# A decoder layer's token mixer: split weights kept in DRAM for the later blocks

## The chip, the cores and the metric

The kernel runs on one core of one Trainium2 chip. The metric is the time of one execution on the device in microseconds (us), the median over runs. Engines are called TensorE (PE in the profile, PEld for its weight loads), VectorE (DVE), ScalarE (ACT), GpSimd (POOL) and SyncE (SP). DVE, ACT, PE and POOL compute; SP only issues DMA transfers, and POOL's queue is used for stores.

## The reference

One layer on x of 2048 tokens and 1024 features, float32, conditioned by a vector c that gives shifts, scales and gates (`mod`, from `mod_w`):

```python
h = modulate(rms_norm(x, norm1_g), shift1, scale1)
q, k, v, g, cb, cc, cx = split(h @ w_in)                 # 4 x 512 and 3 x 512 columns
q, k = rotary(q, positions), rotary(k, positions)
y_ret = group_rms_norm(retention_chunkwise(q, k, v)) * silu(g)
y_conv = group_rms_norm(cb * causal_dwconv(cc * cx))
x = x + gate1 * (concat(y_ret, y_conv) @ w_out)
h = modulate(rms_norm(x, norm2_g), shift2, scale2)
a, val = split(h @ w_up)
x = x + gate2 * ((silu(causal_dwconv(a) + b) * val) @ w_down)
return modulate(rms_norm(x, final_norm_g), *fmod)
```

## The kernel before

**Products in two parts.** x is held as [feature, token]. A float32 operand of the large products is the exact sum of two float32r parts, hi and lo, and a product is three matmuls, hi x hi, hi x lo and lo x hi, accumulated in PSUM (`mm3`, L232 to L236). So each weight has to be split before it is used. `split_w` (L83) does it for a piece of 128 x 1024: SP loads 512 KB into one of 3 `raw` tiles (L85, L86), ScalarE casts it into the first half of one of 4 `w` tiles (L88), and VectorE subtracts the cast from the raw piece into the second half (L89):

```python
raw = rawp.tile([128, 1024], F32, tag="raw", name=nm("raw"))
nc.sync.dma_start(raw, src)
w = whlp.tile([128, 2, 1024], F32R, tag="w", name=nm("w"))
S.copy(w[:, 0, :], raw)
V.tensor_tensor(w[:, 1, :], raw, w[:, 0, :].bitcast(F32), op=ALU.subtract)
```

**The order of the pieces.** `plan` (L93) lists all pieces in the order in which the products take them, and `get_w` splits up to two pieces ahead of the one that it hands out (`ahead`, one in the prologue). The token mixer goes through 4 blocks of 512 tokens (`for b in range(NB)`), and each block uses all its weights again: `w_tok` in 16 pieces (q, k, v and gate, four each), `w_conv` in 12, `w_out` in 8. The pieces of k in block 0 are not in the plan; they are split at L562 to L566 into activation tiles of their own. A piece is 24 large matmuls. The channel mixer after it runs in two halves of 1024 tokens with `w_up` and `w_down`.

**One block.** v, k and q are projected (`proj_step`, L330), v is scaled (L319), k and q are rotated on VectorE straight out of PSUM (`rotary`, L302, its last step a product at L312 to L314), the gate comes out of ScalarE. Then four chunks of retention (`Retention`) alternate with four groups of the short convolution (`Conv`). In `values` the product of k and v goes into the PSUM tile `misc` (L399), which the transposes of the chunk before held until `back` has read it on ScalarE (L433) and VectorE (L434). While this runs, x of the next block is loaded (L500), squared (L211, L212), and its norm taken. `out_proj` (L474) multiplies by `w_out` in two groups of four banks. After each group VectorE takes the sums out of the banks and adds them to x (`xr`, loaded at L479, added at L489), POOL stores the result (L490). Between its 8 weight pieces `spread` (L605) places the normalised chunks of the next block's h: L229 multiplies x by the factor, L222 shifts on ScalarE, L215 and L216 split into `act`; and `more_mod` (L593), which loads four pieces of `mod_w` (L598) and sums them on VectorE (L163, then L165, L166, L170). The next block's first product needs the bank that the first L489 frees. In block 0 the modulation is computed first, with loads at L509 and the same L163, between the first products.

**Who sets the order.** Each engine works through its own list in order. The Tile framework's scheduler makes the lists from priorities, that is from the place in the program, and from the waits on tiles; only the prologue (L513) is written in a fixed order. SP's loads stand in one list too: one that waits for a free tile holds up those behind it.

## Time and profile before

| | |
|---|---|
| runs | 2412.23, 2409.52, 2411.40 us, median 2411.4 |
| span of the profiled execution | 2410.9 us (0.5 under the median) |
| TensorE, its weight loads | 2374.5 and 1953.8 us busy |
| VectorE | 1496.7 us busy |
| ScalarE | 837.1 us busy |
| POOL | 31.8 us busy |
| DMA | 239.53 MB, mean 99 GB/s |
| DMA share by 40 slices of 60 us, tenths | 8444633554264327311111111112511111111102 |

The span runs from the first to the last instruction that the profiler recorded; it is the profiled execution's own time, and the runs are other executions of the same kernel. The token mixer is the first 960 us, some 16 of the 40 slices; the rest is the channel mixer. In the rows, "<-" after an idle time names what ended it. PEclk is the granted clock of TensorE as a share of full speed. The mean of one matmul is larger than the distance of two starts, since they overlap; from a row of windows the count shows the pace.

### The profile page before, as it was taken

What the parts mean: (1) busy time and instruction counts of PE and PEld (TensorE: products, weight loads), DVE (VectorE), ACT (ScalarE), POOL (GpSimd) and SP (SyncE); (2) the same over time, 40 slices, a digit from 0 to 9 for tenths busy, and PEclk for the clock granted to TensorE, in tenths of its full rate; (3) what the DMA queues carried; (4) which work ended last, traced back from release to release, by engine and by line L of the source; (5) the groups of instructions that cost most, each with busy time, mean ns of one, the idle gap of its engine ahead of it and who ended that gap; (6) DMA issues with size and microseconds to landing.
All of it is one profiled execution on the core that took longest, in us unless ns stands there. A gap on an engine that the chain in (4) does not pass through costs nothing.

```text
span 2410.9 us, 27983 instructions
## 1 busy us (share of the span) xinstructions
PE 2374.5 (98%) x10954; PEld 1953.8 (81%) x10954; DVE 1496.7 (62%) x2755; ACT 837.1 (35%) x1234; POOL 31.8 (1%) x66
## 2 busy tenths in 40 slices
PE   8999999999999999999999999999999999999997
PEld 5888888887878887888888888888888888888887
DVE  8999759866986688644444444448844444444436
ACT  5255325523552355322222222234622222222234
POOL 0000000000000000000000000000100000000000
PEclk9999999999999999999999999999999999999999
DMA  8444633554264327311111111112511111111102
GB/s 306 143 131 131 232 113 114 175 187 142 71 216 150 114 86 268 101 53 53 41 47 53 53 36 52 53 53 71 191 54 45 43 53 53 44 44 53 53 27 71
DMA packets 88660, 239.53 MB, mean 99 GB/s; under 512 B 10240, under 2 KB 12304, under 8 KB 88528
## 3 DMA queue, kind: packets, MB, share of 16 engines
q1 hardware_dynamic: 84096, 223.71, 28.6%
q0 software_dynamic: 4288, 13.91, 1.5%
q8 instruction: 86, 1.41, 0.2%
q14 instruction: 46, 0.38, 0.0%
q10 hardware_dynamic: 144, 0.13, 0.0%
HBM read 219.88 MB, written 17.83 MB: 99 GB/s over the span
## 4 chain that ended last, share of the span: by engine, by line
PE 86%; DVE 7%; DMA 4%; issue 2%; ACT 1%; SPq 0%; POOL 0%; DVEq 0%; ACTq 0%; POOLq 0%
PE mm L234 20%; PE mm L236 20%; PE mm L235 20%; PE sc L234 4%; PE sc L235 4%; PE sc L236 4%; DMA x<-in_x 2%; PE y L234 2%; PE y L235 2%; PE y L236 2%; PE misc L234 2%; PE misc L235 2%; PE misc L236 2%; DMA x<-in_mod_w 1%; DVE w L89 1%
## 5 line engine op out<-in xcount | busy, mean ns | idle before, releaser
L234 PE MATMUL mm<-act,w 128*128 128x512 f32 x2048 | 801.7, 391 | 1.7 <-DVE xr L489 1.5
L235 PE MATMUL mm<-act,w 128*128 128x512 f32 x2048 | 798.4, 390 | 1.1 <-DVE act L216 1.1
L236 PE MATMUL mm<-act,w 128*128 128x512 f32 x2048 | 797.5, 389 | 0.0
L88 ACT CAST w<-raw 128x1024 fp32r<-128x1024 f32 x271 | 282.4, 1049 | 668.7 <-issue 362.9
L234 PEld LDWEIGHTS mm<-act,w 128*128 128x128 f32 x2048 | 384.8, 188 | 82.6 <-ACT act L215 3.4
L235 PEld LDWEIGHTS mm<-act,w 128*128 128x128 f32 x2048 | 384.8, 188 | 81.0 <-DVE act L216 2.1
L236 PEld LDWEIGHTS mm<-act,w 128*128 128x128 f32 x2048 | 384.7, 188 | 80.5
L89 DVE TENSOR_TENSOR w<-raw,w 128x1024 fp32r<-128x1024 f32 x271 | 328.4, 1220 | 120.8 <-ACT w L88 120.6
L234 PE MATMUL mm<-w,act 128*128 128x512 f32 x480 | 188.6, 394 | 8.3 <-DVE xr L489 4.4
L235 PE MATMUL mm<-w,act 128*128 128x512 f32 x480 | 188.0, 392 | 0.0
L236 PE MATMUL mm<-w,act 128*128 128x512 f32 x480 | 187.3, 393 | 0.0
L756 DVE SCALAR_TENSOR_TENSOR acc<-sc,mod,acc 128x512 f32<-128x512 f32 (+1 forms) x172 | 126.7, 737 | 83.3 <-PE sc L236 82.8
L729 DVE SCALAR_TENSOR_TENSOR fi<-a,cp,fi 128x512 f32<-128x512 f32 x88 | 66.1, 751 | 173.1 <-ACT fi L728 173.1
L741 DVE TENSOR_TENSOR fi<-fi,mm 128x512 f32<-128x512 f32 x88 | 60.5, 687 | 168.0 <-PE mm L236 167.3
L726 ACT COPY a<-mm 128x512 f32<-128x512 f32 x88 | 51.6, 587 | 316.1 <-PE mm L236 316.1
L235 PE MATMUL sc<-g,w 128*128 128x512 f32 (+1 forms) x348 | 134.4, 386 | 0.0
L234 PE MATMUL sc<-g,w 128*128 128x512 f32 (+1 forms) x348 | 134.4, 386 | 0.0
L236 PE MATMUL sc<-g,w 128*128 128x512 f32 (+1 forms) x348 | 134.3, 386 | 0.0
L234 PEld LDWEIGHTS mm<-w,act 128*128 128x128 f32 x480 | 90.5, 189 | 30.7 <-ACT act L215 10.3
L236 PEld LDWEIGHTS mm<-w,act 128*128 128x128 f32 x480 | 90.9, 189 | 19.2
L235 PEld LDWEIGHTS mm<-w,act 128*128 128x128 f32 x480 | 90.7, 189 | 19.0 <-DVE w L539 0.5
L732 DVE COPY ah<-a 128x2 f32<-128x2 f32 x44 | 7.4, 169 | 156.2 <-ACT a L726 156.2
(225 smaller groups left out, 2814.9 us busy)
## 6 DMA issues: line engine op xcount, KB each, us to landing
raw<-in_w_up SPq DMA_DIRECT2D x88, 512.0 KB, 3.6
raw<-in_w_tok SPq DMA_DIRECT2D x64, 512.0 KB, 5.3
x<-in_mod_w SPq DMA_DIRECT2D x96, 256.0 KB, 4.1
raw<-in_w_conv SPq DMA_DIRECT2D x48, 512.0 KB, 3.6
raw<-in_w_down SPq DMA_DIRECT2D x44, 512.0 KB, 3.6
raw<-in_w_out SPq DMA_DIRECT2D x32, 512.0 KB, 3.5
x<-in_x SPq DMA_DIRECT2D x56, 256.0 KB, 4.2
mw<-in_mod_w SPq DMA_DIRECT2D x32, 256.0 KB, 5.0
```

Source lines behind the costliest of these rows:

```text
L88: S.copy(w[:, 0, :], raw)
L89: V.tensor_tensor(w[:, 1, :], raw, w[:, 0, :].bitcast(F32), op=ALU.subtract)
L234: T.matmul(out, lhs[0], rhs[0], start=first, stop=False)
L235: T.matmul(out, lhs[0], rhs[1], start=False, stop=False)
L236: T.matmul(out, lhs[1], rhs[0], start=False, stop=last)
L726: S.copy(at[:, 2 + o : 514 + o], pa)
L729: V.scalar_tensor_tensor(cv, at[:, 1 + o : 513 + o], fcw[:, j, 1:2], cv, op0=ALU.mult, op1=ALU.add)
L732: V.tensor_copy(ah[:, j, :], at[:, 512 + o : 514 + o])
L741: V.tensor_tensor(sl, sl, pv, op=ALU.mult)
L756: V.scalar_tensor_tensor(acc[s][m][:, cs], ps, gate_of(1, m), acc[s][m][:, cs], op0=ALU.mult, op1=ALU.add)
```

## The change

A piece that the plan holds more than once, of `w_tok`, `w_conv` or `w_out`, is stored in DRAM after its first split, both parts together, 128 x 2048 float32 = 1 MB, by a DMA on POOL's queue (`keep_w`). When the plan comes to it again, SP loads these 1 MB straight into a `w` tile, with no raw tile, cast or subtract. The pieces of k are stored in block 1, where they first go through `split_w`. That is 36 stores and 104 loads; the other pieces of the plan are split as before. The first piece, split in the prologue, is stored by a call of its own.

```diff
-    def split_w(src):
-        """a [128,1024] piece of a weight -> [128, 2, 1024] (hi, lo)"""
+    kept = {}
+
+    def flat2(ap):
+        return ap.rearrange("p a b -> p (a b)").bitcast(F32)
+
+    def split_w(key):
+
+        if key in kept:
+            w = whlp.tile([128, 2, 1024], F32R, tag="w", name=nm("w"))
+            nc.sync.dma_start(flat2(w), kept[key])
+            return w
+        src = a[key[0]][key[1:]]
         raw = rawp.tile([128, 1024], F32, tag="raw", name=nm("raw"))
         nc.sync.dma_start(raw, src)
         w = whlp.tile([128, 2, 1024], F32R, tag="w", name=nm("w"))
         S.copy(w[:, 0, :], raw)
         V.tensor_tensor(w[:, 1, :], raw, w[:, 0, :].bitcast(F32), op=ALU.subtract)
+        keep_w(key, w)
         return w
 
-    # ------------------------------------------- weights, split ahead of their products
+    def keep_w(key, w):
+        if plan.count(key) > 1 and key[0] in KEEP:
+            kept[key] = dram.tile([128, 2048], F32, tag="_".join(map(str, key)), name="_".join(map(str, key)))
+            nc.gpsimd.dma_start(kept[key], flat2(w))
+
+    KEEP = ("w_tok", "w_conv", "w_out")
...
             p = plan[len(made)]
-            made.append(split_w(a[p[0]][p[1:]]))
+            made.append(split_w(p))
...
     made.append(w)
+    keep_w(plan[0], w)
     taken[0] = 1
```

Lines behind the new functions stand 17 to 20 further down in the changed kernel: L163 becomes L182, L216 L235, L229 L248, L399 L418, L489 L508, L490 L509; a kept piece is loaded at L93 and stored at L107.

POOL's list in block 0, before: after the last tile is set to zero come the stores of the first output projection.

```order
L585 MEMSET S_649 128x512
L585 MEMSET S_650 128x512
L490 DMA x_0_0_93<-xr_1967 128x512
L490 DMA x_0_1_94<-xr_1969 128x512
L490 DMA x_0_2_95<-xr_1971 128x512
L490 DMA x_0_3_96<-xr_1973 128x512
```

POOL's list at the same place with the change:

```order
L605 MEMSET S_659 128x512
L605 MEMSET S_660 128x512
L107 DMA w_tok_0_260<-w_209 128x2048
L107 DMA w_tok_1_386<-w_383 128x2048
L107 DMA w_tok_2_393<-w_390 128x2048
L107 DMA w_tok_3_494<-w_491 128x2048
L107 DMA w_tok_0_595<-w_592 128x2048
L107 DMA w_tok_1_766<-w_763 128x2048
```

The stores of the split pieces stand ahead of those of x, one for each piece of block 0 in the order of the splits; the first group of x stores comes after 30 of them.

VectorE's list at the end of block 1's output projection, before. `xr_4136` is the first bank's sum of the second group; `act_4284` is the last chunk of h for block 2, `w_4342` a piece of that block's first weight.

```order
L163 SCALAR_TENSOR_TENSOR x_4241,s_4234<-x_4241,cact 128x512
L163 SCALAR_TENSOR_TENSOR x_4244,s_4234<-x_4244,cact 128x512
L165 TENSOR_TENSOR mod<-s_4234 128x2
L229 TENSOR_TENSOR fo_4281<-x_4279,ss_3312 128x512
L166 TENSOR_TENSOR mod<-mod,cp 128x2
L170 SCALAR_TENSOR_TENSOR amul<-mod,cp 128x1
L89 TENSOR_TENSOR w_4342<-raw_4340,w_4342 128x1024
L489 SCALAR_TENSOR_TENSOR xr_4136<-mm_4132,mod,xr_4136 128x512
L216 TENSOR_TENSOR act_4284<-fo_4281,act_4284 128x512
L489 SCALAR_TENSOR_TENSOR xr_4138<-mm_4133,mod,xr_4138 128x512
```

VectorE's list at the same place with the change, where `act_4257` is that last chunk and `xr_4118` the first sum:

```order
L182 SCALAR_TENSOR_TENSOR x_4217,s_4210<-x_4217,cact 128x512
L182 SCALAR_TENSOR_TENSOR x_4220,s_4210<-x_4220,cact 128x512
L184 TENSOR_TENSOR mod<-s_4210 128x2
L248 TENSOR_TENSOR fo_4254<-x_4252,ss_3333 128x512
L185 TENSOR_TENSOR mod<-mod,cp 128x2
L189 SCALAR_TENSOR_TENSOR amul<-mod,cp 128x1
L235 TENSOR_TENSOR act_4257<-fo_4254,act_4257 128x512
L508 SCALAR_TENSOR_TENSOR xr_4118<-mm_4114,mod,xr_4118 128x512
L508 SCALAR_TENSOR_TENSOR xr_4120<-mm_4115,mod,xr_4120 128x512
```

The split of the weight is gone from between the modulation step and the first sum, and the last chunk's L216, now L235, stands ahead of both sums.

TensorE's list in block 1, before, at the product of k and v of a chunk (`misc`, L399):

```order
L393 MATMUL y_3269<-v_2497,P_3204 128x64
L393 MATMUL y_3269<-v_2497,P_3206 128x64
L234 MATMUL mm_3356<-act_2060,w_3158 128x512
L235 MATMUL mm_3356<-act_2060,w_3158 128x512
L236 MATMUL mm_3356<-act_2060,w_3158 128x512
L234 MATMUL mm_3356<-act_2068,w_3158 128x512
L235 MATMUL mm_3356<-act_2068,w_3158 128x512
L236 MATMUL mm_3356<-act_2068,w_3158 128x512
L399 MATMUL misc_3282<-v_2497,k_2679 128x128 x4
L234 MATMUL mm_3356<-act_2105,w_3158 128x512
L235 MATMUL mm_3356<-act_2105,w_3158 128x512
```

TensorE's list at the same place with the change:

```order
L412 MATMUL y_3290<-v_2553,P_3228 128x64
L412 MATMUL y_3290<-v_2553,P_3230 128x64
L418 MATMUL misc_3303<-v_2553,k_2733 128x128 x4
L253 MATMUL mm_3374<-act_2116,w_3183 128x512
L254 MATMUL mm_3374<-act_2116,w_3183 128x512
L255 MATMUL mm_3374<-act_2116,w_3183 128x512
L253 MATMUL mm_3374<-act_2124,w_3183 128x512
L254 MATMUL mm_3374<-act_2124,w_3183 128x512
L255 MATMUL mm_3374<-act_2124,w_3183 128x512
```

The product of k and v, now L418, stands ahead of six of the large matmuls that it followed; this is so at seven places in the blocks after the first, and TensorE's list is otherwise the same.

## Rows read from the trace of the kernel before

**Rows 1.** The page, part 1: engine, busy us (share of the span) xinstructions.

```profile
PE 2374.5 (98%) x10954; PEld 1953.8 (81%) x10954; DVE 1496.7 (62%) x2755; ACT 837.1 (35%) x1234; POOL 31.8 (1%) x66
```

**Rows 2.** Waits of TensorE from 100 to 1000 us: us in total, times, longest us.

```profile
PE misc L399 <- DVE act L434: 7.0, 3, 2.8
PE mm L234 <- DVE xr L489: 5.9, 4, 2.0
PE mm L235 <- DVE act L216: 1.1, 3, 0.5
```

**Rows 3.** Windows: us, busy (x) of PE, PEld, DVE, ACT, POOL, then PEclk, DMA share, GB/s.

```profile
15.00:20.00 5.00, 5.00 (x16) 2.42 (x14) 4.86 (x18) 0.30 (x1) 0.00 (x0) 0.81 1.04 389
25.00:55.00 30.00, 27.52 (x115) 22.26 (x114) 30.00 (x87) 15.10 (x22) 0.00 (x0) 0.94 0.84 293
55.00:75.00 20.00, 20.00 (x90) 16.57 (x89) 18.09 (x55) 5.23 (x8) 0.00 (x0) 1.00 0.86 297
140.00:150.00 10.00, 7.59 (x34) 6.46 (x34) 9.09 (x17) 4.81 (x9) 0.00 (x0) 0.83 0.46 142
245.00:955.00 710.00, 699.38 (x3454) 582.11 (x3453) 539.50 (x1122) 300.65 (x447) 16.74 (x31) 1.00 0.47 153
250.00:260.00 10.00, 9.12 (x41) 7.27 (x40) 9.93 (x20) 4.91 (x8) 2.16 (x4) 1.00 0.92 318
470.00:480.00 10.00, 10.00 (x46) 8.26 (x45) 6.53 (x18) 3.54 (x4) 0.00 (x0) 1.00 0.90 295
710.00:720.00 10.00, 8.07 (x29) 6.51 (x29) 10.00 (x18) 5.87 (x9) 2.16 (x4) 0.83 0.82 284
```

**Rows 4.** VectorE in order of time, 52 to 73 us: start us, us, instruction [idle <-releaser].

```profile
52.78 1.22 DVE L89 TENSOR_TENSOR w<-raw,w 128x1024 fp32r<-128x1024 f32 x1
...
64.89 1.21 DVE L89 TENSOR_TENSOR w<-raw,w 128x1024 fp32r<-128x1024 f32 x1
...
72.50 0.70 DVE L163 SCALAR_TENSOR_TENSOR x<-x,cact 128x512 f32<-128x512 f32 x1 [1.04 <-DMA x<-in_mod_w]
```

**Rows 5.** TensorE in order of time: products that waited, 82 to 712 us.

```profile
82.35 0.47 PE L234 MATMUL mm<-w,act 128*128 128x512 f32 x1 [0.45 <-DVE fi L312]
...
143.02 1.90 PE L399 MATMUL misc<-v,k 128*128 128x128 f32 x8 [2.41 <-DVE act L434]
...
482.35 0.47 PE L234 MATMUL mm<-w,act 128*128 128x512 f32 x1 [1.51 <-DVE xr L489]
...
711.93 0.47 PE L234 MATMUL mm<-w,act 128*128 128x512 f32 x1 [2.03 <-DVE xr L489]
```

**Rows 6.** The page, part 5, the split on VectorE: busy, mean ns of one | idle before, releaser.

```profile
L89 DVE TENSOR_TENSOR w<-raw,w 128x1024 fp32r<-128x1024 f32 x271 | 328.4, 1220 | 120.8 <-ACT w L88 120.6
```

**Rows 7.** ScalarE in order of time, before 140 us.

```profile
138.08 0.63 ACT L211 ACTIVATE fo<-x 128x512 f32<-128x512 f32 x1 [1.32 <-DMA x<-in_x]
```

**Rows 8.** VectorE in order of time, the end of block 1, 479 to 482 us.

```profile
479.44 0.69 DVE L229 TENSOR_TENSOR fo<-x,ss 128x512 f32<-128x512 f32 x1
...
480.31 1.23 DVE L89 TENSOR_TENSOR w<-raw,w 128x1024 fp32r<-128x1024 f32 x1
481.46 0.75 DVE L489 SCALAR_TENSOR_TENSOR xr<-mm,mod,xr 128x512 f32<-128x512 f32 x1
```

**Rows 9.** ScalarE in order of time, at the same place.

```profile
481.01 0.62 ACT L215 CAST act<-fo 128x512 fp32r<-128x512 f32 x1
```

**Rows 10.** VectorE in order of time, before the L399 of 373 us.

```profile
371.63 1.22 DVE L89 TENSOR_TENSOR w<-raw,w 128x1024 fp32r<-128x1024 f32 x1
372.76 0.35 DVE L434 SCALAR_TENSOR_TENSOR act<-misc,cp,act 128x128 fp32r<-128x128 f32 x1
```

**Rows 11.** Line L490: its 32 stores, from issue to landing.

```profile
DMA to landing us min/median/max: 2.3/5.5/7.9
```

**Rows 12.** The page, part 6: xcount, KB each, median us from issue to landing.

```profile
raw<-in_w_tok SPq DMA_DIRECT2D x64, 512.0 KB, 5.3
```

**Rows 13.** SP's queue, waits from 240 to 960 us: us in total, times, longest us.

```profile
SPq L479 <- DMA x<-xr: 49.5, 19, 7.5
```

## The prediction, made before the changed kernel was run

> **What bounds the kernel now.** The page's busy line comes first [rows 1]: TensorE is busy for 98% of the span of 2410.9 us, VectorE for 62%, ScalarE for 35%. A change that takes work off VectorE and ScalarE can win no more than the time in which TensorE stands still, so the next view is what TensorE waits for. The token mixer's later blocks and the way into the channel mixer hold 7.0 us of waits of L399 on the VectorE step L434, 5.9 us of waits of a new block's first product on L489, and 1.1 us on L216 [rows 2]: 14.0 us. The clock adds to it: in 140 to 150 us and again in 710 to 720 us the granted clock is 0.83 on average [rows 3], which is some time at the lower of the two levels (1.2 instead of 2.4 GHz), each just after a pause of 2 us or more (2.41 before 143.02 us, 2.03 before 711.93 [rows 5]), and costs 10 x 0.17 = 1.7 us. Of the 14.0 us, 2.4 are that wait at 140 us, in block 0, where every weight is still split as before. So **what can be won is 14.0 - 2.4 + 1.7 = some 13 us**, half a per cent of the time, and only if every wait goes.
>
> The third view is DMA by windows [rows 3]. From 245 to 955 us the DMA engines are busy for 47% and there is room. In block 0 there is not: 84% from 25 to 55 us and 86% from 55 to 75 us. The fullest window, 15 to 20 us, moved 389 GB/s, which I take as the ceiling. VectorE is busy for all of 25 to 55 us. The fourth view, VectorE in order of time, shows what the transfers decide there [rows 4]: at 72.50 us VectorE has waited 1.04 us for a DMA of mod_w, and the rotary steps that free TensorE's banks come behind it in the same queue; TensorE then waits 0.45 us for the last of them at 82.35 us [rows 5]. There is no slack between that DMA and TensorE.
>
> **What the change takes away.** 104 of the 271 splits go. A subtract at L89 takes 1.22 us [rows 6], so VectorE loses 104 x 1.22 = 127 us of work, and ScalarE the same number of casts. Nothing of it falls into block 0 before its output projection. By the first view it is worth only what it shortens of the 13 us.
>
> **What it adds.** 36 stores of 128 x 2048 float32 = 1.05 MB on POOL's queue, 32 of them in block 0, and 104 loads that are twice as large as before: 37.7 + 54.5 = 92 MB on top of 239.5. At 389 GB/s one store fills all DMA engines for 1.05 / 0.389 = 2.7 us, and a kept load takes 1.35 us more than the raw one. An issue takes little of POOL: four stores of L490 are 2.16 us in 250 to 260 us [rows 3], 0.54 each, and POOL is busy for 1% [rows 1], so its own time is costed at nothing. If POOL were late, only the stores would be, and they have until the next block.
>
> **Term 1, block 0 up to 100 us: +4 us.** A store follows its subtract. The four from 52.78 to 64.89 us, whose first and last are shown [rows 4], end 1.22 us later and send off 4 x 1.05 = 4.2 MB between 54 and 66 us. The window 55 to 75 us moved 297 x 20 = 5.9 MB of the 389 x 20 = 7.8 MB that fit, so the room is 1.9 MB and 2.3 MB are left over: 6.0 us of all engines. If only the stores give way it costs nothing; if the loads take all of it, 6.0. Two of the four stores start before the loads that VectorE waits for, so I take two thirds, 4 us, and it reaches TensorE whole, since nothing between the DMA and TensorE has slack [rows 4, 5]. From 25 to 55 us it is 293 x 30 = 8.8 MB of 11.7 and again four stores: 1.3 MB over, 3.4 us. VectorE shows no wait for a load there, so I take nothing. Ends of the term: 0 and 9.4. A gain is excluded, since no instruction is removed here.
>
> **Term 2, the wait at 140 us: +1 us.** ScalarE's L433, which feeds L434 and so L399, is queued behind squares that wait for x: 1.32 us for the first [rows 7]. At one piece of a weight in 5.3 us (24 products of 0.222, from 90 in the 20 us of 55 to 75 us [rows 3]) a store falls beside these loads too. Ends: 0, and 4 for one store and a half.
>
> **Term 3, the boundaries at 253 and 936 us: +1.5.** The waits on L489 are 5.9 us in four [rows 2]; without those of 1.51 and 2.03 at 480 and 709 us [rows 5] these two hold 2.4. At 253 us the split between the last modulation step and the first L489 goes; but 250 to 260 us runs at 318 GB/s and a share of 0.92 [rows 3] and is given two stores and larger loads: +1. At 936 us L216 and a split both stand before L489 in the new order, and the split is one of the channel mixer's, which stays: +0.5. Ends: -2.4, if both stalls go, and +9.4, two stores (5.4) and the 4 of the next term.
>
> **Term 4, the boundaries at 480 and 709 us: +1.5 us each, +3.** This is where a reader would expect the gain. In the trace L89 stands between L229 and L489: L229 at 479.44, L89 at 480.31, L489 at 481.46 [rows 8], and TensorE waited 1.51 us for that L489 and 2.03 at 709 us [rows 5]. The new order has no L89 there, but L216 of the last chunk has moved up in its place, ahead of L489. L216 needs ScalarE's L222 and L215, which follow L229: L215 starts at 481.01 and takes 0.62 [rows 9], so L216 can start at 481.63, and L489 some 0.60 later at 482.23, which is 0.8 later than before. The stall isn't removed, its cause changes from a split to a chain over ScalarE. Above it VectorE works through the last modulation loads and the last chunk of x as they land, with the DMA engines at 0.90 in 470 to 480 us [rows 3], and the weight load ahead of these in SP's queue is now twice as long: 1.35 if the queue is full, nothing if not; I take 0.7. Ends: -3.5, if both stalls go, and +4 each, 0.8 and the 2.7 of one whole kept load in front.
>
> **Term 5, L399 in the later blocks: -1.4.** Of the 7.0 us [rows 2] the wait in block 0 is 2.4; 4.6 are left, 2.8 the longest and 1.8 before 373 us. There L89, 1.22 us long, stands right before the last L434 [rows 10]; it goes, and a cast ahead of L433 goes as well. But TensorE now has L399 six products earlier: at 0.222 each that is 1.33 us less cover. I take -0.7 at each of the two, half of what the split and an equal part of the cast's place would give. Ends: -4.6 (both gone) and +2.7 (no relief counts, twice 1.33).
>
> **Term 6, the clock: +1.7.** With pauses of 4 us at 82 and of 3 at 480 I expect one more stretch at the low level, at the measured 1.7. Ends: -1.7 and +5 (three more).
>
> **Sum:** 4 + 1 + 1.5 + 3 - 1.4 + 1.7 = +9.8 us on the span of 2410.9, 2420.7; the span lies 0.5 under the median of the runs, so 2421.2, given as **2421 us**. All lower ends together are -12.2, all upper ends +38.5.
>
> **A rule on the stores.** Between 250 and 260 us four stores of L490 took 0.54 us of POOL each while VectorE was busy for 9.93 of 10 us [rows 3], and the 32 land in 2.3 to 7.9 us [rows 11]; that speaks against POOL being held up. The Trainium skill, SBUF — State Buffer, section "SBUF: two separate sides", says the opposite can happen: a DMA issued from GpSimd has its descriptors written by that engine, and while VectorE runs an instruction in a 2-port mode it is locked out, so that the transfer starves. By that rule stores would not compete with the loads of block 0 while VectorE is busy, and terms 1 and 2 would fall away; the row bears it out little.
>
> **The rivals.**
> - *Relief wins.* The DMA engines' idle half takes the stores, terms 1 and 2 are nil, the boundary stalls go: 2411 - 12 = about 2400. For it: mean DMA share 0.47 [rows 3] and 127 us less of VectorE. Against: the stalls stand where the DMA is at 0.9, and the order puts a new chain in place of the split. 0.14.
> - *They cancel.* Terms 1 and 2 are as forecast, or halved, and terms 3, 4 and 5 win 3 to 5 us: about 2411. 0.20.
> - *Kept loads come late.* There are four w tiles, so a kept load can start only when TensorE has finished the piece four before: three pieces of 24 x 0.222 = 5.3 us ahead, 16.0 us. It decides from a landing later than that. A raw load of w_tok lands in 5.3 us [rows 12], so 6.7 with 1.35 more; SP's queue held up behind L479 for at most 7.5 us [rows 13] makes 14.2, still inside. If it fails at three boundaries, with two loads each 5 us late: +30, 2441. 0.06.
> - *Stores starve.* POOL gets a store out only where VectorE leaves room, and VectorE is busy for 30.00 of the 30 us from 25 to 55 us [rows 3], so the stores slip behind the loads: terms 1 and 2 out, 9.8 - 5 = +4.8, 2416. 0.04.
>
> That the change doesn't do what it says is no rival: the new order holds the 36 stores and 104 loads.
>
> **How the numbers follow.** The forecast of contention over relief has 0.56. Two tenths of a per cent, 4.8 us, is about what a measurement of this kernel can tell. Slower by more: 0.56 + 0.06 = 0.62; within: 0.20 + 0.04 = 0.24; faster: 0.14. The range reaches from 2404, where over half of the relief rival's 12 us comes, to 2437, where terms 1 and 4 stand at their upper ends (9.4 and 8 in place of 4 and 3) and the clock falls three times more (2421 + 5.4 + 5 + 3.3 = 2435). The forecast's own range is 2415 to 2437.
>
> **What would show it.** Right: DMA share near 1.0 and VectorE's wait for mod_w at 72 us grown to 3 us or more; the stall at 82 us at about 4 us; L489 waits of 2 to 4 us at 480 and 709 us with L216 ahead; L399 waits shorter by 1 us in all. Wrong: no new TensorE stall under 150 us (term 1), boundary stalls under 1 us (term 4), or TensorE waiting for a w DMA in a later block (the third rival).

## The result: 1.6% slower

The changed kernel takes 2449.31 us (median of 4 runs, 2443.49 to 2452.06) against 2410.77 us before in the same comparison: a ratio of 1.016, 95% interval 1.0143 to 1.0177, or +38.5 us. The forecast was 2421, the range 2404 to 2437. The direction was right, the size was nearly four times too small, and the time lies outside the range.

The changed kernel's page, its busy line, which answers to [rows 1]:

```profile
PE 2383.5 (97%) x10954; PEld 1960.2 (80%) x10954; DVE 1388.0 (57%) x2651; ACT 739.7 (30%) x1130; POOL 51.0 (2%) x102
```

VectorE lost 109 us and ScalarE 97 us of work, and TensorE waits longer all the same. The waits of TensorE in the first 1000 us (us in total, times, longest):

```profile
PE mm L253 <- DVE xr L508: 15.8, 5, 6.4
PE mm L253 <- DVE fi L331: 7.9, 1, 7.9
PE misc L418 <- DVE act L453: 7.8, 5, 5.1
PE mm L253 <- ACT act L234: 5.8, 4, 2.5
```

L508 is the old L489, L418 the old L399. Against [rows 2] the waits on the freed bank (L508) grew from 5.9 to 15.8 us; the one on the rotary step (L331), 0.45 us in [rows 5], is 7.9 us. TensorE in order of time shows the six longest waits of the token mixer behind its prologue:

```profile
93.45 0.77 PE L253 MATMUL mm<-w,act 128*128 128x512 f32 x1 [7.92 <-DVE fi L331]
...
159.95 2.08 PE L418 MATMUL misc<-v,k 128*128 128x128 f32 x8 [5.09 <-DVE act L453]
...
275.52 0.79 PE L253 MATMUL mm<-w,act 128*128 128x512 f32 x1 [4.63 <-DVE xr L508]
...
510.54 0.76 PE L253 MATMUL mm<-w,act 128*128 128x512 f32 x1 [6.41 <-DVE xr L508]
...
744.64 0.76 PE L253 MATMUL mm<-w,act 128*128 128x512 f32 x1 [2.57 <-issue]
...
972.91 0.61 PE L253 MATMUL mm<-act,w 128*128 128x512 f32 x1 [4.19 <-DVE xr L508]
```

In time, the first product of block 1 starts at 275.52 us instead of 254.52, so 21 us are lost by the end of block 0; at 510.54 us the lag is 28.2 (482.35 before), at 744.64 it is 32.7 (711.93), at 972.91 it is 35.3 (937.62), and at the end of the span 38.7 (2449.6 and 2410.9 us).

Windows of the changed kernel, columns as in [rows 3], first of block 0, then 10 us from each of the six waits on:

```profile
25.00:55.00 30.00, 26.21 (x107) 20.61 (x106) 27.46 (x79) 11.81 (x17) 1.61 (x3) 0.94 1.02 399
55.00:75.00 20.00, 18.93 (x84) 15.20 (x83) 17.27 (x47) 7.71 (x10) 2.16 (x4) 1.00 0.96 363
75.00:85.00 10.00, 10.00 (x46) 8.29 (x45) 3.21 (x13) 0.31 (x1) 0.00 (x0) 1.00 0.97 391
93.45:103.45 10.00, 10.00 (x32) 8.03 (x33) 6.97 (x17) 3.16 (x3) 1.06 (x2) 0.71 0.36 104
159.95:169.95 10.00, 10.00 (x43) 8.57 (x44) 9.47 (x26) 3.60 (x7) 1.07 (x2) 0.79 0.69 227
275.52:285.52 10.00, 10.00 (x34) 8.08 (x35) 6.70 (x10) 4.49 (x7) 2.17 (x4) 0.77 1.01 401
510.54:520.54 10.00, 10.00 (x33) 8.04 (x34) 8.34 (x18) 3.08 (x5) 2.16 (x4) 0.74 0.87 327
744.64:754.64 10.00, 10.00 (x38) 8.12 (x39) 7.48 (x15) 3.08 (x5) 2.16 (x4) 0.84 1.03 393
972.91:982.91 10.00, 10.00 (x37) 8.09 (x38) 5.64 (x8) 3.97 (x6) 2.16 (x4) 0.83 0.95 316
```

The DMA engines are full for 25 to 85 us (shares of 0.96 to 1.02, 363 to 399 GB/s, where the prediction took 389 as the most that fits); VectorE, which was busy for all of 25 to 55 us, now stands still for 2.5 of the 30. What that does to the loads shows in their time from issue to landing between 25 and 85 us (xcount, KB each, median us), before:

```profile
raw<-in_w_tok SPq DMA_DIRECT2D x10, 512.0 KB, 5.1
x<-in_mod_w SPq DMA_DIRECT2D x12, 256.0 KB, 5.5
```

With the change:

```profile
w_tok<-w POOLq DMA_DIRECT2D x7, 1024.0 KB, 8.3
raw<-in_w_tok SPq DMA_DIRECT2D x11, 512.0 KB, 8.4
x<-in_mod_w SPq DMA_DIRECT2D x11, 256.0 KB, 9.5
```

These loads take 3 to 4 us longer. And each of the six waits is followed by some us at the lower clock: 0.71, 0.79, 0.77, 0.74, 0.84 and 0.83 of the full clock over 10 us cost 10 x (0.29 + 0.21 + 0.23 + 0.26 + 0.16 + 0.17) = 13.2 us, where before two such stretches cost 3.4 [rows 3].

ScalarE at a split in block 0, then VectorE in block 0 and at the end of block 1, in order of time:

```profile
44.64 1.05 ACT L99 CAST w<-raw 128x1024 fp32r<-128x1024 f32 x1 [8.01 <-DMA raw<-in_w_tok]
```

```profile
83.60 0.69 DVE L182 SCALAR_TENSOR_TENSOR x<-x,cact 128x512 f32<-128x512 f32 x1 [6.58 <-DMA x<-in_mod_w]
...
499.35 0.69 DVE L248 TENSOR_TENSOR fo<-x,ss 128x512 f32<-128x512 f32 x1 [10.49 <-DMA x<-in_x]
...
506.06 0.69 DVE L182 SCALAR_TENSOR_TENSOR x<-x,cact 128x512 f32<-128x512 f32 x1 [3.18 <-DMA x<-in_mod_w]
...
509.09 0.69 DVE L235 TENSOR_TENSOR act<-fo,act 128x512 fp32r<-128x512 f32 x1 [1.27 <-ACT act L234]
509.70 1.40 DVE L508 SCALAR_TENSOR_TENSOR xr<-mm,mod,xr 128x512 f32<-128x512 f32 x2
```

The 1.04 us that VectorE waited for mod_w [rows 4] are 6.58 us, and ScalarE, which waited at most 1.62 us for a piece of w_tok at this place before, waits 8.01. At the end of block 1 VectorE waits 10.49 us for a chunk of x, 3.18 us for mod_w, and 1.27 us for ScalarE before the L235 that the new order puts ahead of L508; that is the chain of term 4, behind late loads. The loads are late there since the stores of x1 in front of them are: those stores, beside a kept load, land in 3.7 to 9.6 us (2.3 to 5.2 at this place before), each load of xr waits for one of them, and x and mod_w stand behind. SP's list at this place, and, over all, the landing of the stores of x1 and the waits of SP's queue for them from 262 to 1000 us (us in total, times, longest):

```profile
482.41 0.33 SPq L93 DMA_DIRECT2D w<-w_out  x1
484.91 8.82 SPq L498 DMA_DIRECT2D xr<-in_x  x4
493.82 0.38 SPq L519 DMA_DIRECT2D x<-in_x  x1
```

```profile
DMA to landing us min/median/max: 2.3/7.0/9.6
```

```profile
SPq L498 <- DMA x<-xr: 26.9, 11, 8.7
```

The median landing of a store of x1 went from 5.5 us [rows 11] to 7.0, the longest from 7.9 to 9.6, and the loads of xr, which wait for the stores to free their tiles, hold up what stands behind them in SP's queue for up to 8.7 us at a time (7.5 before [rows 13]). Summed from 240 to 960 us these waits are fewer than before, 34.0 us in 14 against 49.5 in 19, so if they cost time, it is not by their sum but by where the long ones fall.

### The profile page after: what moved, and what is told of

Read it like the earlier page. It is cut to its first block, busy times and chain, and to the rows that moved or that the text cites. A ratio compares the mean times of both kernels' runs of the same rounds, so it can differ in the third digit from the quotient of the medians.

```text
span 2449.6 us, 27730 instructions
## 1 busy us (share of the span) xinstructions
PE 2383.5 (97%) x10954; PEld 1960.2 (80%) x10954; DVE 1388.0 (57%) x2651; ACT 739.7 (30%) x1130; POOL 51.0 (2%) x102
## 4 chain that ended last, share of the span: by engine, by line
PE 62%; issue 29%; DVE 4%; DMA 3%; POOL 1%; ACT 1%; SPq 0%; POOLq 0%; DVEq 0%; ACTq 0%
PE mm L253 14%; PE mm L254 14%; PE mm L255 14%; PE sc L255 3%; PE sc L254 3%; PE sc L253 3%; PE y L254 2%; PE y L255 2%; PE y L253 2%; PE misc L253 2%; PE misc L254 2%; PE misc L255 2%; DMA x<-in_mod_w 1%; DMA x<-in_x 1%; POOL x L509 1%
## 5 line engine op out<-in xcount | busy, mean ns | idle before, releaser
L99 ACT CAST w<-raw 128x1024 fp32r<-128x1024 f32 x167 | 173.3, 1048 | 504.6 <-issue 347.0
L253 PE MATMUL mm<-w,act 128*128 128x512 f32 x480 | 191.9, 401 | 27.3 <-DVE xr L508 11.0
L100 DVE TENSOR_TENSOR w<-raw,w 128x1024 fp32r<-128x1024 f32 x167 | 202.4, 1222 | 25.5 <-ACT w L99 25.3
L254 PE MATMUL mm<-w,act 128*128 128x512 f32 x480 | 190.7, 397 | 0.0
L255 PE MATMUL mm<-w,act 128*128 128x512 f32 x480 | 190.1, 399 | 0.0
L253 PEld LDWEIGHTS mm<-w,act 128*128 128x128 f32 x480 | 92.4, 193 | 50.6 <-issue 18.1
L255 PEld LDWEIGHTS mm<-w,act 128*128 128x128 f32 x480 | 92.5, 193 | 20.3 <-DVE act L235 0.5
L254 PEld LDWEIGHTS mm<-w,act 128*128 128x128 f32 x480 | 92.5, 193 | 19.5 <-DVE w L558 0.5
```

What stands on the lines that cost most here:

```text
L253: T.matmul(out, lhs[0], rhs[0], start=first, stop=False)
L254: T.matmul(out, lhs[0], rhs[1], start=False, stop=False)
L255: T.matmul(out, lhs[1], rhs[0], start=False, stop=last)
```

## The experiments

Two theories at first. **Transfers**: the stores fill the DMA in block 0, and the kept loads at the boundaries. **Lists**: taking the splits out lets the scheduler put other work ahead of L489, and the moved lists cost the time. All times are medians; each run has its own runs of the kernel before beside it, and their medians lie between 2407.55 and 2410.77 us, so a difference of 2 or 3 us between two experiments can be theirs.

### The stores alone

```diff
     def split_w(key):
-        if key in kept:
...
     def keep_w(key, w):
-        if plan.count(key) > 1 and key[0] in KEEP:
+        if plan.count(key) > 1 and key[0] in KEEP and key not in kept:
```

> The 36 stores stay, but nothing is read back: every later block splits its raw weights as before. Theory T (transfers): the loss of block 0, 21 us up to the first product of block 1 (275.5 against 254.5 us), is the stores' alone and stays; the later blocks run as before: 2411 + 21 = 2432 us. Rival O (the moved instruction lists cost it, not the transfers): with the splits back the lists are nearly the old ones, 2411 to 2415. Rival S (the stores slow everything, the larger loads are innocent): near 2449.

Measured: 2435.03 us against 2409.79, +25.2, ratio 1.0106 (1.0091 to 1.0121). Its waits of VectorE from 60 to 90 us, and its first product of block 1:

```profile
DVE x L178 <- DMA x<-in_mod_w: 8.6, 2, 6.6
```

```profile
276.05 0.77 PE L249 MATMUL mm<-w,act 128*128 128x512 f32 x1 [5.49 <-DVE xr L504]
```

The 6.6 us for mod_w and the 21 us by the end of block 0 are all there. **Two thirds of the loss are the stores'**, and 21.5 of these 25.2 us are there by the end of block 0.

### The loads alone

```diff
-            kept[key] = dram.tile([128, 2048], F32, tag="_".join(map(str, key)), name="_".join(map(str, key)))
-            nc.gpsimd.dma_start(kept[key], flat2(w))
+            kept[key] = True
+            if key == ("w_conv", 0, 1):
+                kept[0] = dram.tile([128, 2048], F32, tag="one", name="one")
+                nc.gpsimd.dma_start(kept[0], flat2(w))
```

and the load reads `kept[0]`, so that every kept load brings the same piece. The one store fell at 101.9 us, where the DMA share was 0.39 and not near idle.

> One store only (the first piece of w_conv, at about 98 us, where the DMA is idle), and all 104 kept loads read that 1 MB: the weights of the later blocks are the wrong ones, the loads have their full size and time. Theory T: block 0 as before, the stalls at the three later boundaries as in the changed kernel, +14 to +18: 2425 to 2429. Rival S: about 2411. Rival O: +14 to +18 as well, which the next kernel parts from T.

Measured: 2422.90 us, +13.1, ratio 1.0052 (1.0035 to 1.0069), a little under Theory T. With the stores' 25.2 this makes 38.3 of the 38.5: within the noise the two parts add. VectorE at the end of block 1 (L237 is the old L216, L510 the old L489) has the list of the changed kernel, with no modulation step between the last chunk's split and the sum:

```profile
485.23 0.16 DVE L191 SCALAR_TENSOR_TENSOR amul<-mod,cp 128x1 f32<-128x1 f32 x1
486.65 0.69 DVE L237 TENSOR_TENSOR act<-fo,act 128x512 fp32r<-128x512 f32 x1 [1.27 <-ACT act L236]
487.26 1.40 DVE L510 SCALAR_TENSOR_TENSOR xr<-mm,mod,xr 128x512 f32<-128x512 f32 x2
```

Ahead of these VectorE waits 1.92 us for mod_w and 1.07 us for x, and TensorE waits 5.05 us here.

### Loads of the old size, no split

```diff
-            nc.sync.dma_start(flat2(w), kept[0])
-            return w
+            nc.sync.dma_start(w[:, 0, :].bitcast(F32), kept[0][:, 0:1024])
+            return w[:, 0:1, :].broadcast_to([128, 2, 1024])
```

> As the kernel with one store, but a kept load brings 512 KB, the hi part alone, and the products take it for both parts: no split in the later blocks and no more bytes than before. What is computed is only the hi part of one piece. Theory T: this is the relief by itself, the boundary stalls shrink to 0 to 2 us each: 2399 to 2411, I take 2406. Rival O: the lists are those of the changed kernel, so the later blocks lose 14 to 18 still: 2425 to 2429.

Measured: 2418.54 us, +8.7, ratio 1.0039 (1.0024 to 1.0053), between the two ranges; both expectations missed. What I took for a gain is a loss even without larger loads. VectorE at the end of block 1 in this run (L184 is the old L163, L510 the old L489):

```profile
479.31 0.69 DVE L237 TENSOR_TENSOR act<-fo,act 128x512 fp32r<-128x512 f32 x1 [1.27 <-ACT act L236]
481.01 0.69 DVE L184 SCALAR_TENSOR_TENSOR x<-x,cact 128x512 f32<-128x512 f32 x1 [1.01 <-DMA x<-in_mod_w]
...
481.67 0.69 DVE L184 SCALAR_TENSOR_TENSOR x<-x,cact 128x512 f32<-128x512 f32 x1
...
482.32 0.69 DVE L184 SCALAR_TENSOR_TENSOR x<-x,cact 128x512 f32<-128x512 f32 x1
...
482.96 0.69 DVE L184 SCALAR_TENSOR_TENSOR x<-x,cact 128x512 f32<-128x512 f32 x1
...
483.82 1.41 DVE L510 SCALAR_TENSOR_TENSOR xr<-mm,mod,xr 128x512 f32<-128x512 f32 x2
```

Four modulation steps of the next block stand ahead of L510 now, the first waiting 1.01 us for its load; TensorE was through with the bank at about 480 us and gets it at 484.67. The same four steps stand ahead of the sum at the end of block 2; in the changed kernel and with the loads alone they stand behind it at both places. So this run has a list of its own, and its 8.7 us are that list's. The 4.4 us between it and the loads alone are therefore not the price of the larger loads, and how the 13.1 us of the loads alone divide between late loads and the list is not shown. Why the scheduler filled this place here and not there is not shown either.

### The stores of w_tok later

```diff
+    splits = {}
+
     def keep_w(key, w):
-        if plan.count(key) > 1 and key[0] in KEEP:
+        splits[key] = splits.get(key, 0) + 1
+        if plan.count(key) > 1 and key[0] in KEEP and (key[0] != "w_tok" or key[1] == 1 or splits[key] > 1):
```

> The 12 pieces of w_tok that block 0 splits are split again in block 1 and stored there; 20 stores stay in block 0. Theory T: the VectorE wait of 6.6 us for mod_w at 83.6 us and TensorE's 7.9 us at 93 us go, with the smaller ones at 45 and 57 us and the slow clock after them, 13 us in all; 12 more stores in block 1, where DMA is at about half, cost 0 to 5: 2436 to 2441. Rival O: no change, 2449.

Measured: 2435.28 us, +25.5, ratio 1.0112 (1.0097 to 1.0127). As the transfers have it, and just under their range: from 25 to 85 us a load of mod_w lands in 5.2 us again and one of w_tok in 4.9, and the waits of the first 100 us go; those of 4.74 us before 145.29 (L399) and 7.04 us before 264.19 (L489), beside the stores of w_conv and w_out, stay.

### Only w_conv kept

```diff
-    KEEP = ("w_tok", "w_conv", "w_out")
+    KEEP = ("w_conv",)
```

> Only the 12 pieces of w_conv are kept: 12 stores in block 0 between about 98 and 190 us, where the DMA was busy for 37%, and 36 kept loads that all fall beside the retention, away from the boundaries. Theory T+O (stores in a full DMA, larger loads at the boundaries, and the boundary's list): most of the loss is gone, what stays is the L399 wait at 155 us, where a store meets the loads of x: 2411 to 2420. If every store and load costs its share of the bytes (a third of them), the loss is a third of 38: 2424.

Measured: 2416.07 us, +7.9 on the medians, ratio 1.0025 (1.0011 to 1.0039). Inside the first range: a third of the bytes costs less than a third of the loss. The wait of L399 in block 0, beside the stores, grew from 2.41 to 4.29 us. The waits on L489 are 6.5 us in four (5.9 [rows 2]); those on L399 in the later blocks, where the splits beside it are gone, fell from 4.6 to 3.0 us, less than block 0 lost.

### The loads of xr on POOL's queue

```diff
-                nc.sync.dma_start(xr[m], xT(b, 4 * mg + m))
+                nc.gpsimd.dma_start(xr[m], xT(b, 4 * mg + m))
```

> The changed kernel with the loads of xr moved from SP's queue to POOL's. In the changed kernel the stores of x1 land in 8 to 10 us at the end of block 1, beside a kept load, the xr loads wait for them at the head of SP's queue until 493.4 us, and x and mod_w come behind them. Theory H (head of the queue): the last loads start some 8 us earlier, the boundary stalls of 5 to 6 us fall to 1 to 2, 2436 to 2441. If the DMA engines themselves are the limit there: 2447 to 2451.

Measured: 2442.86 us, ratio to before 1.0143 (1.0128 to 1.0158). That is 6.4 us under the change's median, but the intervals of the two ratios overlap, and with each run's own kernel before the difference is 3.9 us. It falls between the two expectations: the waits at the ends of blocks 1 and 3 went from 6.41 and 4.19 to 3.27 and 1.04 us, those at the ends of blocks 0 and 2 rose, to 7.07 and 3.57. By the waits the head of SP's queue is part of it at two of the four boundaries; the times do not tell it from noise.

### L489 first

The last chunk of x and the second modulation step of each output projection are traced behind the last L489 (in block 3 behind the first), with an order edge on VectorE.

```diff
+                if mm == (7 if b < 3 else 4):
+                    with tc.issue_after(add.ins):
+                        late()
...
-        cut = ((), (0, 1), (2, 3), (4,), (5,), (6,), (7,), ())
+        cut = ((), (0, 1), (2, 3), (4,), (5,), (6,), (), ())
...
-                             more_mod() if i in (4, 5) else None) for i in range(8)]
+                             more_mod() if i == 4 else None) for i in range(8)], lambda: (chunk(7), more_mod())
```

> The changed kernel, with the last chunk of x (its load, L229, L222, L215, L216) and the second modulation step of each output projection put behind the four last L489 on VectorE (behind the first of them in block 3). Theory O (what stands before L489 on VectorE sets the boundary): the stalls at 270, 504, 742 and 968 us, 18 us in all, fall to under 1 us each and the slow clock after them goes too: 2424 to 2432. If the bank is not what TensorE waits for: 2445 to 2451.

> The same edit on the kernel before: its four boundary stalls are 5.9 us with 1.7 us of slow clock; under Theory O 2402 to 2406, otherwise 2411.

Measured: 2438.66 us on the change (ratio 1.0126, 1.011 to 1.0142), and on the kernel before 2414.10 (1.0022, 1.0008 to 1.0035): slower. Both expectations missed. The waits on L489 fell, to 2.8 us in three in the changed kernel, and came back one projection later, there once and in the kernel before three times (2.87, 2.99 and 2.28 us). TensorE one projection into block 1, in the changed kernel with the edit:

```profile
300.54 0.77 PE L253 MATMUL mm<-w,act 128*128 128x512 f32 x1 [6.83 <-DVE v L338]
```

L338 is scaled_v, which frees the banks of v and stood behind the delayed modulation, and that waits for its loads (2.99, 1.44 and 2.01 us from 291 to 298 us). What has to be late must not only stand behind L489, its loads have to be there.

### One step moved: the last chunk's split

```diff
+                if mm == 7 and b < 3:
+                    with tc.issue_after(add.ins):
+                        late.pop()()
...
+                if k < 7:
+                    hn.append(shift_split(t, 0, k))
+                else:
+                    late.append(lambda: hn.append(shift_split(t, 0, k)))
```

> The changed kernel with one thing moved: the shift and split of the last chunk of x (L222, L215, L216) stands behind the last L489 in blocks 0 to 2, nothing else. If the chain over ScalarE ahead of L489 is what the prediction's term 4 said, each of these boundaries wins the 1.3 us of waiting and the 0.6 of L216, 4 to 6 us in all: 2443 to 2445. If the late loads of mod_w and x alone set L489: 2448 to 2450.

Measured: 2441.61 us, ratio 1.0133 (1.0116 to 1.015). That is 7.7 us under the change's median, and 5.9 under it when each is held against its own runs of the kernel before (+32.7 and +38.5), inside the 4 to 6 expected. The waits at the ends of blocks 1 and 2 went from 6.41 and 2.57 to 2.70 and 1.72 us, and no slow clock follows them. The chain over ScalarE in term 4 is real, and with the clock it cost some 2 us at each of the three boundaries, not 0.8.

### The modulation away from the boundaries

In blocks 1 to 3 the two modulation steps of the output projection go to the second and third convolution group, and no step may stand ahead of the last L489. The steps take their loads of mod_w with them, so this move by itself does not tell the list from late loads.

```diff
-                             more_mod() if i in (4, 5) else None) for i in range(8)]
+                             more_mod() if i in (4, 5) and b == 0 else None) for i in range(8)]
...
-                if j == 0:
+                if j == 0 or b > 0:
                     more_mod()
```

On the half-size load, on the kernel before, on w_conv kept, and on the full change:

> The half-size load once more (hi part of one piece, no split in the later blocks, no more bytes), with the modulation taken away from the boundaries: in blocks 1 to 3 the two steps of the output projection go to the second and third convolution group, and no step of the next block may stand ahead of the last L489. Theory O2 (in the half-size run the modulation that the scheduler pulled ahead of L489, with its DMA waits, costs the boundaries what the missing splits win): the stalls of 4.7, 4.0 and 2.7 us at 480, 713 and 941 us fall to 1 to 2 each, and the run is 6 to 12 us shorter than with the half-size load alone, 2406 to 2412, at best under the kernel before. If the loss there has another source: 2416 to 2420.

> The same move of the modulation in the kernel before, with all its splits: the boundary stalls at 480 and 709 us (1.5 and 2.0 us, 1.7 us of slow clock) should fall to about 1 us, while VectorE gets 16 us of work more in the convolution groups of blocks 1 and 2, whose L399 waits may grow by as much as they win: 2403 to 2411.

> Only w_conv kept, with the same move: VectorE has lost the splits of the convolution groups and takes the modulation instead. The boundaries have the splits of w_tok and w_out as before. Left are the L399 wait of 4.6 us at 140 us where the stores meet the loads of x (2.2 more than before, and 1.7 of slow clock), and nothing else that is new: 2404 to 2412, against 2416 with w_conv kept alone.

> The full change (36 stores, 104 loads of 1 MB) with the modulation moved as in the other runs. If the parts add, stores 25.2 us, larger loads 4.4 us and moved lists 8.7 us, and the move is worth 5.2 us beyond these, this run is 2409 + 25.2 + 4.4 - 5.2 = 2433 us. If the lists cost little in the full change, where late loads rule the boundaries, it stays at 2440 or above.

Measured: 2403.79 us (ratio 0.9979, 0.9969 to 0.9988), 2403.71 (0.9979, 0.9969 to 0.9988), 2410.72 (1.0004, 0.9995 to 1.0014) and 2433.08 us (1.0096, 1.0074 to 1.0118). The three stalls of the half-size run, 4.28, 3.64 and 2.29 us in its trace, are gone: no wait on L489 is left there after block 0. That run becomes 14.7 us shorter by this move alone (13.9 with each run's own kernel before): what it had lost, and more. The full change becomes some 16 us shorter, and the one wait on L508 that is left after 240 us is of 3.5 us, at the end of block 0. It comes out at the 2433 that the sum of the parts gave; that two of these parts, 8.7 and 4.4, come from a run with another list makes the agreement partly luck, and its four runs spread from 2426.58 to 2437.21. And **with the modulation moved alike, the run without splits and the kernel with all of them are equal**, though their lists are not quite: L399 still stands earlier on TensorE where the splits are gone.

### L399 held behind more products

```diff
+            if k == 1:
+                for m in kv_mm:
+                    tc.add_manual_dep(m.ins, o.ins.name, mybir.DependencyInfo(
+                        mybir.DependencyClass.NoSync, mybir.DependencyReason.DATA), reason="behind")
```

in `feat_mm`, for the four products of L399 that were traced before; `k == 4` holds them behind 15 products. The kernel before has L399 behind six products at four of the seven places named above and behind 13 or 15 at the other three, so six does not bring back all of its cover. On the half-size load with the modulation moved (six, then 15), and on the kernel before with it (15):

> The half-size load with the modulation moved (2403.8 us), and the four products of L399 held on TensorE behind the first six products of the next convolution piece, where the kernel before has most of them. Theory P (the relief was given back by L399's earlier place): its waits, 6.9 us in six, fall to under 3, and the run is 3 to 5 us shorter, 2399 to 2401. Theory N (nothing to win from the freed VectorE): 2403 to 2405.

> The same with L399 behind 15 products instead of six, 3.3 us later: no L399 wait should be left, 2396 to 2399. Beside the next run, which has the splits and the same lists, the difference is the relief alone: Theory N 0 to 1 us, Theory P 2 to 4 us.

> The kernel before with all its splits, the modulation moved (2403.7 us) and L399 behind 15 products. Its L399 waits are 6.1 us in three, with 1.7 us of slow clock twice; 15 products cover 3.3 us, so they go: 2396 to 2399 under both theories; 2400 to 2402 if the splits hold VectorE up elsewhere once L399 does not.

Measured: 2404.55 (ratio 0.9983, 0.9972 to 0.9995), 2400.60 (0.9964, 0.9951 to 0.9977) and 2399.89 us (0.996, 0.9945 to 0.9975). Theory P falls: with six products the waits of L399 are 1.3 us in two, and the run is not shorter. With 15 products they are gone from both runs, which now have the same order of products on TensorE but for one, and both take the same time again, 1 to 2 us over the 2396 to 2399 expected. The last two runs' waits of TensorE from 100 to 1000 us; first without splits:

```profile
PE misc L200 <- DVE S L436: 3.0, 5, 1.2
PE mm L255 <- DVE xr L517: 1.6, 1, 1.6
PE y L421 <- DVE P L410: 1.5, 2, 0.8
```

And with all splits:

```profile
PE mm L234 <- DVE xr L496: 1.7, 1, 1.7
PE y L400 <- DVE P L389: 1.7, 5, 0.8
PE misc L434 <- ACT fo L77: 1.4, 1, 1.4
PE misc L434 <- DVE fi L428: 1.3, 1, 1.3
PE misc L179 <- DVE S L415: 0.2, 1, 0.2
```

Some 6 us of waits are left in each, with VectorE busy for 1378.9 us in the one and 1490.3 in the other. **The relief is worth nothing here that these runs could tell from zero** (2403.79 against 2403.71 us in ten runs each, 2400.60 against 2399.89); the last of these runs, with all splits in place and nothing stored, beats both kernels, the one before by 10.1 us.

### Smaller pieces for the stores

Why did the loads pay for the overflow of block 0? The queue lines give more bytes a packet to the added stores, 37.75 MB in 5184 packets, than to the loads, 223.71 MB in 84096. So the stores alone were run once more in four and in eight pieces:

```diff
-            nc.gpsimd.dma_start(kept[key], flat2(w))
+            for i in range(4):
+                part = slice(512 * i, 512 * (i + 1))
+                nc.gpsimd.dma_start(kept[key][:, part], flat2(w)[:, part])
```

> The stores alone (2435.0 us), each cut into four of 128 x 512, so that a row is 2 KB instead of 8. Same bytes, four issues on POOL instead of one. Theory K (the queues take turns by packet): the loads' share of a full DMA rises from about a quarter to a half, VectorE's wait for mod_w of 6.6 us falls to 2 to 4, the landing of a store grows, and the run is 2418 to 2428. If turns do not depend on the size of a packet: 2432 to 2437.

> The same in eight pieces of 128 x 256, rows of 1 KB. Theory K: the loads get more than the stores, 2414 to 2424, unless so small rows cost the DMA engines more than they give back, then above the run with four pieces. Without Theory K: 2432 or more.

Measured: 2442.74 us (ratio 1.0141, 1.012 to 1.0163) and 2436.62 (1.0124, 1.0109 to 1.0139), where one piece takes 2435.03. The wait for mod_w is 5.3 and 6.2 us at its longest. Theory K finds no support. But the packets became less small than the rows: the pages count 5184 packets more in POOL's queue with one piece, 11520 with four and 13824 with eight, and the 2304 by which the last two differ are all under 512 B. So both runs send the data in the same packets, of about 4 KB instead of 8; smaller ones stay untested, and why the loads pay stays open.

## Why the prediction was right in sign and wrong in size

**What could be won** was put at 13 us at most, and what VectorE loses at what it shortens of them. Right as a bound, and the runs go further: the waits of L399 in the later blocks became 1.9 us shorter (term 5), and that is all. The boundary waits were set by loads and by the list, and the L399 waits, which a cast and a split fed, by the place of L399 on TensorE, which the scheduler moves as soon as the splits go.

**Term 1** (+4, ends 0 and 9.4) is the first step that failed. The mechanism, the place and the instruction were as told: the wait for mod_w at 72 us, then the rotary. But "Two of the four stores start before the loads that VectorE waits for, so I take two thirds" let the stores bear a third of the overflow for nothing. The stores were slowed too (those of the first 75 us land in 7.2 to 11.3 us, the single one of the loads alone in 6.4), but that took nothing off the path: 7.92 - 0.45 = 7.5 us came through to TensorE at 93 us. And "VectorE shows no wait for a load there, so I take nothing" looked at the wrong engine for 25 to 55 us: with 1.3 MB too many ScalarE's cast waited, 8.01 us before 44.64 and 6.24 before 55.71, and TensorE behind it 1.30 us before 47.10 and 1.07 before 58.17 (5.8 us on L234 in all instead of 3.7). Together some 9.6, just over the upper end: the loads paid for the whole overflow. The stores alone show it (6.6 us for mod_w, 21.5 us by the end of block 0), and with the stores of w_tok later these waits go.

**Term 2** (+1) was 5.09 - 2.41 = 2.7, inside its ends; the wait is 4.29 us with the stores of w_conv alone and 1.27 with the loads alone, so it is the stores' as told. **Term 3** (+1.5) was 4.63 - 0.88 at the end of block 0 and 4.19 - 1.46 at the end of block 3, where I had only counted an L216: 6.5, inside its ends of -2.4 and 9.4. The first is the stores' (5.49 us with the stores alone, 1.94 with the loads alone), the second is not (5.04 us with the loads alone). **Term 4** (+3) was 6.41 - 1.51 and 2.57 - 2.03: 5.4, of which 4.9 at the first place, over its upper end of 4, and 0.5 at the second. The chain that it named is in the trace (1.27 us before L235), and moving it alone wins 5.9 us. What it lacked is the loop in front, which the rows at the end of block 1 show: a kept load slows the stores of x1, these hold the loads of xr, and these the last x and mod_w. **Term 5** (-1.4) was 2.7 - 4.6 = -1.9: the one gain, and of the size forecast.

**Term 6** (+1.7, up to 5) is the second step that failed. "I expect one more stretch at the low level" stood beside four pauses that the same sum made longer; all six had one, 13.2 - 3.4 = 9.8 us, a quarter of the loss. Part of that could have been worked out from rows that were there: pauses of 2.41 and 2.03 us had been followed by 1.7 us of loss each [rows 3, 5], which for the new ones at 82 and 480 makes 3.4 and not 1.7. The rest comes from pauses that the other terms had too short or did not expect.

These come to 9.6 + 2.7 + 6.5 + 5.4 - 1.9 + 9.8 = 32.1 of the 38.7 us between the spans; the rest is in smaller waits, 1.9 us of them in the prologue and 1.5 behind the token mixer. Every term but the fifth cost more than the value taken. The first four share a cause in the main, the added transfers, and the sixth follows their pauses, but the range was cut as if they were independent (and its 2437 is 2 us over the sum of 2435 given for it). That all upper ends together make the measured 38.5 is luck: term 6 lies far over its own, terms 2 to 5 under theirs.

**The rivals.** The relief came to no more than term 5. Kept loads did not come late for TensorE: no row of the later blocks shows it waiting for a w load; the wait before 744.64 us has no releaser in the profile ("issue"), but L508 started at 743.79 there, 0.85 us ahead of the product, as it did at 510.54 (0.84). Stores did not starve: they took 0.53 us of POOL each and landed in 5.8 to 11.3 us, also from 25 to 55 us, where VectorE was busy for 27.46 of the 30 us. By the rule of the Trainium skill, SBUF — State Buffer, section "SBUF: two separate sides", they could have been held back; it speaks of VectorE's instructions in a 2-port mode, and no row here shows whether VectorE ran any. What the trace shows is that the loads of SP's queue came late.

## What to carry to other kernels

Work that is taken off an engine is worth only the waits that it ends, and which these are is tested cheaply: leave the work out without paying for it, with the lists of the other engines held as they were, and see whether the time moves at all. Traffic that was added where the DMA was full was paid in full by the loads that someone waits for, and the long pauses that it made on TensorE cost the slow clock after them once more. Where a load is late, look at every engine that takes one, not only at the one that waited before. Where a scheduler makes the lists, a lighter engine can get other work put ahead of the step that frees a bank; compare the lists there before the times of two runs are subtracted.

## What the hardware showed that was not expected

- With the DMA full from 25 to 85 us, eight stores of 1 MB raised the time from issue to landing by 3 to 4 us (loads of mod_w from 5.5 to 9.5, of w_tok from 5.1 to 8.4), and VectorE waited 6.6 us for one of them. Packets of about 4 KB instead of 8 did not change it much (5.3 and 6.2 us).
- The slow clock: six pauses of 2.57 to 7.92 us, six stretches at the low level, which cost 1.6 to 2.9 us each. In the kernel before, the pause of 1.51 us before 482.35 had none, but neither had one of 2.81 us before 602.21, with a granted clock of 1.00 over the 10 us behind each; so not every pause of such a length is followed by one.
